# Sums over places in the pair selection: from folds on VectorE to matmuls with scaled identities on TensorE

## The chip, the cores and the metric

The kernel runs on one core of a Trainium2 chip. The metric is the device time of one execution in microseconds; before the change the median of three runs is 3086.44 us (3086.29 to 3088.57). The engines are named as in the profile: PE is TensorE (PEld its weight loads), DVE is VectorE, ACT is ScalarE, POOL is GpSimd, SP is SyncE, which here only issues DMAs.

## The reference

Two layers of an encoder on 512 tokens of width 1024. Each layer has two kinds of attention, a projection, a layer norm, and then a feed-forward part (PEER) that picks 16 of 16384 one-neuron experts for each token and each of 8 heads. The change touches only this choice:

```python
q = (xc @ wq).reshape(PEER_CHUNK, PEER_HEADS, 2, half)
sc = jnp.einsum('chpd,hpnd->chpn', q, sub_keys, preferred_element_type=jnp.float32)
s1, i1 = lax.top_k(sc[:, :, 0], PEER_TOPK)
s2, i2 = lax.top_k(sc[:, :, 1], PEER_TOPK)
cand = (s1[..., :, None] + s2[..., None, :]).reshape(...)
top_s, pos = lax.top_k(cand, PEER_TOPK)
eidx = jnp.take_along_axis(cidx, pos, axis=-1)
g = jax.nn.softmax(top_s, axis=-1)
```

Each chosen position `pos` among the candidate pairs has to be turned back into two key numbers, i1 and i2.

## The kernel before

The 512 tokens are four chunks of 128. Chunks 1, 2, 3 are "dense" (the experts of a chunk are spread into a table G in DRAM and all experts are computed), chunk 0 is "gathered" (experts fetched by indirect DMA). `order` is 1, 2, 3, 0. In a layer the work runs so:

- Attention; then the queries of the first two chunks together (`sub_keys`, generator `one`), of the third dense chunk (`two`, from `start(1)`) and of chunk 0 (`start(2)`). For each of 8 heads PE computes two queries `ps_pq` (8 fp32 matmuls of 128x128 for a single chunk; the trace has two records for each of them), ACT copies them out (`pq`, L478), PE multiplies them with the keys (`ps_ps`, L443), ACT copies the scores (`psc`, L446). For a dense chunk DVE then takes the best 16 keys of each half (`top_keys`: L496, L498, L501, here "a head").
- The pair selection `top_pairs` of each dense chunk, on DVE with two copies by ACT: 50 candidate sums (`cd`), the best 16 of them (`ts`, `pu`), and then the turning back. `ge` (16 places x 128, fp16) says for each place whether `pos` reaches the place's offset; `t` holds the steps `df` between the key numbers (copied wide by ACT, L563). Their product (L570) summed over the 16 places is i1. The sum is `fold`: three halvings and a last addition (L510, L511). `ge` times a table of steps (L575), folded, gives the offset `of` (L578); a comparison of `of` with the places (L580) times the second key numbers `t` (ACT, L573; DVE, L582), folded, gives i2.
- `gates(c)` (L720 on): PE transposes the gates, i1 and i2 of a chunk (`ps_t`, L727); DVE splits the gates into halves gh and gl; ACT writes i1 and i2 transposed into `iT`.
- `spread`: 48 times, DVE builds one-hot tiles from `iT` (`o12`, `ah`, `al`: L819 to L821), PE multiplies them (`ps_g`, L830, L831: fp16 128x128), ACT copies into staging; between them PE has the first expert blocks (`ps_a`, L772).
- The main loop over 128 expert blocks (L776 to L781 and L964 to L966), PE-heavy, with chunk 0's gathers beside it.

The order of the instructions on each engine is fixed when the program is built: a scheduler puts them in place by a priority, which is the place where the code emits them, and by its own view of when operands are there. Each engine then works through its list. In the code before, `top_pairs(order[2])` is emitted ahead of `start(2)`, the queries of chunk 0. In both orders, as in the trace, the two layers have the same pattern; layer 1's events of this stage come 1524.7 us after layer 0's, and only layer 0 is shown.

Of the kernel before, what the change touches and what calls it, by code (L numbers as in the profile page):

```python
# [8 lines left out]
F32 = mybir.dt.float32  # L9
F32R = mybir.dt.float32r  # L10
F16 = mybir.dt.float16
# [7 lines left out]
P = 128  # L19
# [3 lines left out]
NC = S // P  # L23
L = 2
HD = 64
NE = 16384
NB = 128
PH = 8
TK = 16
J = PH * TK  # L30
# [9 lines left out]
NCAND = [TK // (a + 1) for a in range(TK)]  # L40
# [5 lines left out]
def encoder_kernel(ctx: ExitStack, tc: tile.TileContext, x, ln_in_g, ln_in_b, w_in, qn_g, kn_g, sink,  # L46
# [12 lines left out]
    cp = ctx.enter_context(tc.tile_pool(name="cp", bufs=1))  # L59
# [8 lines left out]
    def acc_bank(nm):  # L68
        return ps.tile([P, 512], F32, tag="acc", name=nm, bufs=6)
# [5 lines left out]
        return ap.to_broadcast(shape)  # L75

    h = cp.tile([P, NC, D], F32, name="h")
    i1f = cp.tile([P, NC, J], F16, name="i1f")
    i2f = cp.tile([P, NC, J], F16, name="i2f")
    gte = cp.tile([P, NC, J], F32, name="gte")  # L80

    def rsqrt(src, scale, eps, n, nm):

# [64 lines left out]
    ident = cp.tile([P, P], F32, name="ident")  # L148
# [4 lines left out]
    v.tensor_copy(iota2, iota4.rearrange("p (n t) -> p n t", t=4)[:, :, 0:2])  # L153
    look = cp.tile([P, 3, TK, 8], F16, name="look")
    nc.sync.dma_start(look.rearrange("p a k j -> p (a k j)"), look_c)
    cos = cp.tile([P, NC, HD], F32, name="cos")
    sin = cp.tile([P, NC, HD], F32, name="sin")
    dist = cp.tile([P, 384], BF16, name="dist")
# [3 lines left out]
    for l in range(L):  # L162
# [41 lines left out]
        order = dense + gat  # L204
# [81 lines left out]
        st = {}  # L286
# [220 lines left out]
        def fold(t, dst):  # L507

            for n in (8, 4, 2):
                v.tensor_tensor(out=t[:, :n, :], in0=t[:, :n, :], in1=t[:, n:2 * n, :], op=ADD)  # L510
            v.tensor_tensor(out=dst, in0=t[:, 0, :], in1=t[:, 1, :], op=ADD)  # L511

        def pair_tiles():
            def small(tag, shape, dt):
                return pt.tile(shape, dt, tag=tag, name=tag, bufs=1)
            return dict(cd=small("cd", [P, PH, NCD], F32), ts=small("ts", [P, PH, TK], F32),
                        pu=small("pu", [P, PH, TK], U32), pos=small("pos", [P, J], F16),
                        xf=small("xf", [P, 2, PH, TK], F16), df=small("df", [P, PH, TK], F16),
                        of=small("of", [P, J], F16),
                        ge=pt.tile([P, TK, J], F16, tag="ge", name="ge"), t1=pt.tile([P, TK, J], F16, tag="t1", name="t1"))  # L520

        def pair_steps(st, c, tl):
# [33 lines left out]
            def table(i):  # L556
                return bc(look[:, i, :, None, :], b8)
# [11 lines left out]
            yield  # L569
            v.tensor_tensor(out=t1, in0=t1, in1=ge, op=MUL)  # L570
            yield
            fold(t1, i1f[:, c, :])
            act.copy(t1v, per_head(xf[:, 1]))  # L573
            yield
            v.tensor_tensor(out=gev, in0=gev, in1=table(1), op=MUL)  # L575
            yield
            fold(ge, of)
            v.tensor_tensor(out=of, in0=pos, in1=of, op=SUB)  # L578
            yield
            v.tensor_tensor(out=gev, in0=wide(of), in1=table(2), op=EQ)  # L580
            yield
            v.tensor_tensor(out=t1, in0=t1, in1=ge, op=MUL)  # L582
            yield
            fold(t1, i2f[:, c, :])
            yield
            gs = sm.tile([P, PH], F32, tag="gs", name="gs")
            v.tensor_reduce(out=gs, in_=gc, axis=AX.X, op=ADD)
# [7 lines left out]
        tks = {}  # L595
        xTs = {}

        groups = order[:2], order[2:3], order[3:]
# [121 lines left out]
        def gates(c):  # L720

            b = acc_bank("ps_t")
            i12 = ga.tile([P, 2, P], F32, tag="i12", name="i12", bufs=1)
            v.tensor_copy(i12[:, 0], i1f[:, c, :])
            v.tensor_copy(i12[:, 1], i2f[:, c, :])
            for i, src in enumerate((gte[:, c, :], i12[:, 0], i12[:, 1])):
                pe.transpose(b[:, i * P:(i + 1) * P], src, ident)  # L727
# [4 lines left out]
            iT = ga.tile([P, P // 8, 2, 8], F16, tag="iT", name="iT", bufs=3)  # L732
# [4 lines left out]
            act.copy(iT.rearrange("p o a t -> p a o t"), b[:, P:3 * P].rearrange("p (a o t) -> p a o t", a=2, t=8))  # L737
            flat[c] = gh, glf, gl, iT
# [140 lines left out]
        for c in gat:  # L879
# [3 lines left out]
            def rank(c=c, idx=idx, fx=fx):  # L883
                sx = slot()
                n = 2 * PH * TK
                st = {k: t.rearrange("p (a h k) -> p a h k", a=2, h=PH)
                      for k, t in (("sv", sx[:, :n]), ("ix", sx[:, n:2 * n].bitcast(U32)))}
                sc = []
                for i in range(2):
                    t = slot().rearrange("p (h a n) -> p h a n", a=2, n=P)  # L890
                    nc.sync.dma_start(t, Q[:, i * 4:(i + 1) * 4])
                    sc.append(t)
                yield
                for hd in range(PH):
                    yield from top_keys(st, hd, sc[hd // 4][:, hd % 4])
                big = [slot() for _ in range(3)]
                tl = dict(ge=big[0].bitcast(F16), t1=big[1].bitcast(F16))
                tl = {k: t.rearrange("p (a j) -> p a j", a=TK) for k, t in tl.items()}
                o = 0
                for k, shp, dt in (("cd", [PH, NCD], F32), ("ts", [PH, TK], F32), ("pu", [PH, TK], U32), ("pos", [J], F16),  # L900
                                   ("xf", [2, PH, TK], F16), ("df", [PH, TK], F16), ("of", [J], F16)):
                    n = math.prod(shp) // (2 if dt == F16 else 1)
                    t = big[2][:, o:o + n]
                    t = t if dt == F32 else t.bitcast(dt)
                    ax = "abc"[:len(shp)]
                    if len(shp) > 1:
# [4 lines left out]
                v.tensor_scalar(fx, i1f[:, c, :], 128.0, float(l * NE), op0=MUL, op1=ADD)  # L911
                v.tensor_tensor(out=idx, in0=fx, in1=i2f[:, c, :], op=ADD)  # L912
# [185 lines left out]
```

## Time and profile before

| | |
|---|---|
| median of three runs | 3086.44 us |
| the profiled execution | 3086.3 us |
| its span in the trace | 3084.5 us |
| PE busy | 2989.5 us (97%) |
| DVE busy | 2453.0 us (80%) |
| ACT busy | 1311.1 us (43%) |

A line of a timeline gives start, busy time, engine, source line, output <- input, shapes, count, and in brackets the idle time ahead of it with what ended it. Busy times on PE include a pipelined end, so the step from one start to the next is what an instruction takes in a row of its kind. [...]

### The profile page before, as it was taken

The page shows a single profiled execution, that of the slowest core. Times are in us where ns is not written, and L with a number is a line of the kernel's source. Part 1 is how long each engine was busy: PE and PEld are TensorE (multiplying, and loading weights), DVE is VectorE, ACT ScalarE, POOL GpSimd, SP SyncE. Part 2 cuts the span into 40 slices and gives each one's busy share as a digit, 9 for nine tenths or more (in the row PEclk, how much of TensorE's full clock was granted, in tenths as well). Part 3 has the DMA queues.
Part 4 walks back from the last instruction along what each step waited for, and adds up shares of the span by engine and source line. Part 5 has one row for each costly group of instructions (what it writes and reads, how often), then busy time and mean ns, then how long its engine had stood idle before and what let it go on. Part 6 is the DMA issues. An engine that isn't in the chain of part 4 may idle for free. (4 is left out here: it accounts for less than half of the span.)

```text
span 3084.5 us, 47606 instructions
## 1 busy us (share of the span) xinstructions
PE 2989.5 (97%) x17858; PEld 2704.7 (88%) x17858; DVE 2453.0 (80%) x5207; ACT 1311.1 (43%) x2586; POOL 748.8 (24%) x524
## 2 busy tenths in 40 slices
PE   6999899999999999999999999999999999999998
PEld 6989887899999999999888888779999999999997
DVE  6777999678777777877777779987787787787777
ACT  2664268343333333333347532773433333333332
POOL 0000000014444444444000000000244344444540
PEclk9999999999999999999999999999999999999999
DMA  4113567659888888888520236675698988888882
GB/s 178 42 56 129 212 232 287 219 199 333 317 322 313 320 318 313 320 317 314 189 96 15 71 132 244 245 290 179 246 334 305 325 315 313 322 317 311 324 311 92
DMA packets 262232, 749.46 MB, mean 243 GB/s; under 512 B 19952, under 2 KB 130288, under 8 KB 231792
## 3 DMA queue, kind: packets, MB, share of 16 engines
q1 hardware_dynamic: 188272, 477.94, 42.8%
q0 software_dynamic: 73728, 268.47, 24.1%
q8 instruction: 140, 2.29, 0.3%
q14 instruction: 92, 0.75, 0.1%
HBM read 691.81 MB, written 54.53 MB: 242 GB/s over the span
## 5 line engine op out<-in xcount | busy, mean ns | idle before, releaser
L921 POOL DMA_INDIRECT gt<-in_dram,idx x512 | 742.3, 1450 | 2062.7 <-DVE idx L912 1197.7
L779 PE MATMUL ps_a<-xTh,uh 128*128 128x384 f32 x1824 | 610.6, 335 | 3.7 <-ACT uh L776 3.7
L781 PE MATMUL ps_a<-xTh,ul 128*128 128x384 f32 x1824 | 612.2, 336 | 0.0
L780 PE MATMUL ps_a<-xTl,uh 128*128 128x384 f32 x1824 | 610.8, 335 | 0.0
L966 PE MATMUL ff<-vh,wl 128*128 128x512 f32 x1476 | 576.4, 391 | 0.0
L964 PE MATMUL ff<-vh,wh 128*128 128x512 f32 x1476 | 574.9, 389 | 0.0
L965 PE MATMUL ff<-vl,wh 128*128 128x512 f32 x1476 | 574.5, 389 | 0.0
L997 ACT CAST vh<-vt 128x1024 fp32r<-128x1024 f32 x246 | 258.5, 1052 | 607.8 <-PE ff L966 308.1
L998 DVE TENSOR_TENSOR vl<-vt,vh 128x1024 fp32r<-128x1024 f32 x246 | 301.2, 1224 | 195.8 <-ACT vh L997 194.7
L779 PEld LDWEIGHTS ps_a<-xTh,uh 128*128 128x128 f32 x1824 | 342.7, 188 | 14.4 <-ACT uh L776 5.6
L780 PEld LDWEIGHTS ps_a<-xTl,uh 128*128 128x128 f32 x1824 | 342.6, 188 | 10.4
L927 DVE CUSTOM_DVE_ANT_0 junk<-gt,h 128x1024 bf16<-128x1024 f32 x256 | 313.1, 1223 | 37.6 <-DMA gt<-in_dram,idx 33.0
L781 PEld LDWEIGHTS ps_a<-xTh,ul 128*128 128x128 f32 x1824 | 342.5, 188 | 0.1
L1004 ACT CAST wh<-w 128x384 fp32r<-128x384 f32 x246 | 126.3, 513 | 478.3 <-DVE w L1001 474.3
L938 DVE SCALAR_TENSOR_TENSOR gacc<-gt,gw,gacc 128x1024 f32<-128x1024 f32 x252 | 311.6, 1280 | 21.3 <-DMA gt<-in_dram,idx 21.3
L966 PEld LDWEIGHTS ff<-vh,wl 128*128 128x128 f32 x1476 | 277.2, 188 | 57.6
L964 PEld LDWEIGHTS ff<-vh,wh 128*128 128x128 f32 x1476 | 277.0, 188 | 49.6 <-ACT wh L1004 0.9
L965 PEld LDWEIGHTS ff<-vl,wh 128*128 128x128 f32 x1476 | 277.2, 188 | 48.6
L777 DVE TENSOR_TENSOR ul<-ut,uh 128x1024 fp32r<-128x1024 f32 x228 | 277.9, 1219 | 21.7 <-ACT uh L776 21.7
L776 ACT CAST uh<-ut 128x1024 fp32r<-128x1024 f32 x228 | 239.7, 1052 | 121.8 <-PE ps_a L780 120.5
L1005 DVE TENSOR_TENSOR wl<-w,wh 128x384 fp32r<-128x384 f32 x246 | 137.5, 559 | 158.9 <-ACT wh L1004 158.9
L772 PE MATMUL ps_a<-xTd,ut 128*128 128x384 f32 x448 | 156.1, 493 | 0.0
(261 smaller groups left out, 4857.4 us busy)
## 6 DMA issues: line engine op xcount, KB each, us to landing
ut<-in_dram SPq DMA_DIRECT2D x128, 1024.0 KB, 8.4
vt<-in_dram SPq DMA_DIRECT2D x128, 1024.0 KB, 7.2
w_pq<-in_dram SPq DMA_DIRECT2D x48, 1024.0 KB, 5.0
gg<-G SPq DMA_DIRECT2D x62, 768.0 KB, 13.8
G<-stg SPq DMA_DIRECT2D x24, 1920.0 KB, 7.0
w_o<-in_dram SPq DMA_DIRECT2D x24, 1024.0 KB, 4.8
w_q<-in_dram SPq DMA_DIRECT2D x8, 1024.0 KB, 6.3
gt<-in_dram,idx POOLq DMA_INDIRECT x512, 7.3
```

Source lines behind the costliest of these rows:

```text
L777: v.tensor_tensor(out=ul.rearrange(ff), in0=us, in1=uh.rearrange(ff).bitcast(F32), op=SUB)
L779: pe.matmul(b[:, :ND], uh[:, k, :], xTh[:, k, :], start=k == 0, stop=False)
L780: pe.matmul(b[:, :ND], uh[:, k, :], xTl[:, k, :], start=False, stop=False)
L781: pe.matmul(b[:, :ND], ul[:, k, :], xTh[:, k, :], start=False, stop=k == KD - 1)
L921: pool.indirect_dma_start(out=t, out_offset=None, in_=src, in_offset=bass.IndirectOffsetOnAxis(ap=idx[:, j:j + 1], axis=0))
L927: v.tensor_tensor_reduce(out=jk, in0=t, in1=h[:, c, :], op0=MUL, op1=ADD, scale=1.0, scalar=0.0, accum_out=a_[:, j:j + 1])
L938: v.scalar_tensor_tensor(acc[j % 2], t, w_[:, j:j + 1], acc[j % 2], op0=MUL, op1=ADD)
L964: pe.matmul(b, wh[:, cs], vh[:, ns], start=blk == 0, stop=False)
L965: pe.matmul(b, wh[:, cs], vl[:, ns], start=False, stop=False)
L966: pe.matmul(b, wl[:, cs], vh[:, ns], start=False, stop=blk == NB - 1)
L997: act.copy(vh, vt[:, bi, :])
L998: v.tensor_tensor(out=vl, in0=vt[:, bi, :], in1=vh.bitcast(F32), op=SUB)
```

## The change

For dense chunks the folds go. Seven identities scaled by 1, 2, 3, 4, 5, 8 and 16 are made once at the start (`idw`, fp16). `sum_places` lets PE add the 16 places: 16 matmuls with a place of `t` as weights and the identity as the moving side, into one PSUM tile `ps_f`, which comes out transposed, so that ACT copies it straight into `iT_all`. For `of` 15 matmuls with scaled identities as weights and places of `ge` as the moving side replace the product with the table and its fold. `t2` is a second buffer beside `t1`. The matmuls are emitted at a priority lowered by 400 for the first two chunks and not lowered for the third; the third selection is emitted behind `start(2)`. The transposes of i1 and i2 in `gates` go with the two casts ahead of them. Chunk 0 keeps the old code.

```diff
+    steps_ = [0] + NCAND[:-1]
+    idw = {k: cp.tile([P, P], F16, name=f"id{k}") for k in sorted(set(steps_) - {0})}
+    for k, t in idw.items():
+        v.tensor_scalar(t, ident, float(k), None, op0=MUL)
...
+        def sum_places(t, i, iT, late):
+
+            b = acc_bank("ps_f")
+            with tc.high_priority(offset=-late):
+                for a in range(TK):
+                    pe.matmul(b[:, :P], t[:, a, :], idw[1], start=a == 0, stop=a == TK - 1)
+            act.copy(iT[:, :, i, :], b[:, :P].rearrange("p (o t) -> p o t", t=8))
...
-            fold(t1, i1f[:, c, :])
+            if iT is not None:
+                sum_places(t1, 0, iT, late)
+                b = acc_bank("ps_f")
+                with tc.high_priority(offset=-late):
+                    for a in range(1, TK):
+                        pe.matmul(b[:, :P], idw[steps_[a]], ge[:, a, :], start=a == 1, stop=a == TK - 1)
+                v.tensor_tensor(out=of, in0=pos, in1=b[:, :P], op=SUB)
+                t1 = tl["t2"]
...
+            else:
+                fold(t1, i1f[:, gat.index(c), :])
             act.copy(t1v, per_head(xf[:, 1]))
...
-            fold(t1, i2f[:, c, :])
+            if iT is not None:
+                sum_places(t1, 1, iT, late)
...
         def top_pairs(c):
-            for _ in pair_steps(tks[c], c, pair_tiles()):
+            iTs[c] = iT_all[:, dense.index(c)]
+            for _ in pair_steps(tks[c], c, pair_tiles(), iTs[c], 0 if c == order[2] else 400):
                 pass
...
-        top_pairs(order[2])
         for _ in start(2):
             pass
+        top_pairs(order[2])
         gates(order[2])
```

How the order moves, at three places of layer 0. First PE, in the queries of the third chunk (`two`): here is the program before, where `tr_x0` are the transposes of chunk 0 and `ps_pq` the queries.

```order
L443 MATMUL ps_ps_4282<-keys_4185,pq_4265 128x128
L472 MATMUL ps_pq_4297<-xT1_3674,w_pq_4227 128x128 x8
L129 MATMUL tr_x0_4395<-ident_81,h_69 128x128 x4
L129 MATMUL tr_x0_4401<-ident_81,h_69 128x128 x4
L472 MATMUL ps_pq_4411<-xT1_3674,w_pq_4268 128x128 x8
```

The same place now; `t1_4331` and `t2_4332` are the first chunk's products, `ps_f_4427` the sum that gives its i2.

```order
L534 LDWEIGHTS t1_4331
L534 MATMUL ps_f_4389<-id1_90,t1_4331 128x128
L534 LDWEIGHTS t2_4332
L534 MATMUL ps_f_4427<-id1_90,t2_4332 128x128
L130 MATMUL tr_x0_4450<-ident_82,h_69 128x128 x4
L130 MATMUL tr_x0_4456<-ident_82,h_69 128x128 x4
L478 MATMUL ps_pq_4466<-xT1_3689,w_pq_4283 128x128 x8
L534 LDWEIGHTS t2_4332
```

Of the 16 matmuls of the i2 sum one stands ahead of the transposes and of the queries, 15 behind them; all 31 of the first chunk's other two sums stand ahead as well. Farther down the second chunk's i2 sum stands the same way: one matmul ahead of the query `ps_pq_4618`, 15 much later.

Second DVE, where `t2_4332` is written: now the product stands behind the fourth head of the third chunk (`psc_4480`), and behind all candidates of the second chunk; the second chunk's product, `of`, comparison and product follow in one piece.

```order
L606 TENSOR_TENSOR ge_4330<-of_4329,look_88 128x2048
L504 MAX_INDEX ix_3869<-sv_3868,psc_4480 128x8
L608 TENSOR_TENSOR t2_4332<-t2_4332,ge_4330 128x2048
L560 CAST pos_4495<-pu_4494 128x128
L616 TENSOR_REDUCE gs_4614<-gte_72 128x8
L583 TENSOR_TENSOR ge_4499<-pos_4495,look_88 128x2048
L617 RECIPROCAL gs_4614<-gs_4614 128x8
L585 TENSOR_TENSOR t1_4500<-t1_4500,ge_4499 128x2048
L618 TENSOR_TENSOR gte_72<-gte_72,gs_4614 128x128
L593 TENSOR_TENSOR of_4498<-pos_4495,ps_f_4576 128x128
L606 TENSOR_TENSOR ge_4499<-of_4498,look_88 128x2048
L608 TENSOR_TENSOR t2_4501<-t2_4501,ge_4499 128x2048
```

Before, the first chunk's product stood behind the second head, and the second chunk's candidates behind it.

```order
L498 MAX_INDEX ix_3854<-sv_3853,psc_4244 128x8 x2
L580 TENSOR_TENSOR ge_4315<-of_4314,look_87 128x2048
L589 TENSOR_TENSOR gte_72<-gte_72,gs_4390 128x128
L582 TENSOR_TENSOR t1_4316<-t1_4316,ge_4315 128x2048
L496 MAX sv_3853<-psc_4285 128x8 x2
```

Third PE, at the end of chunk 0's queries (`xT2`): the third chunk's sums come behind the last query.

```order
L478 MATMUL ps_pq_5040<-xT2_4449,w_pq_4992 128x128 x8
L449 MATMUL ps_ps_5051<-keys_4991,pq_5032 128x128
L534 LDWEIGHTS t1_5065
L534 MATMUL ps_f_5123<-id1_90,t1_5065 128x128
L534 LDWEIGHTS t1_5065
L534 MATMUL ps_f_5123<-id1_90,t1_5065 128x128
L592 LDWEIGHTS id16_96
L592 MATMUL ps_f_5141<-ge_5064,id16_96 128x128
L449 MATMUL ps_ps_5051<-keys_4991,pq_5049 128x128
```

Behind them come, in this order, five and then ten matmuls left of the second chunk's i2 sum, the third chunk's i2 sum, the transpose of its gates, the 24 transposes `tr_x` and the spread. In ACT's list the wide copy of the third chunk's `df` stands in the middle of chunk 0's query copies, between `pq_4861` and `pq_4876`.

## Rows read from the trace of the kernel before

**Rows 1.** The page: the chain that ended last, by engine.

```profile
PE 32%; DVE 0%; ACT 0%; DVEq 0%; issue 0%
```

**Rows 2.** Windows of 10 us in the stage of the selections, layer 0.

```profile
370.00:380.00 10.00, 7.46 (x67) 7.27 (x66) 10.00 (x91) 0.88 (x3) 0.00 (x0) 1.00 0.95 359
380.00:390.00 10.00, 7.29 (x46) 6.86 (x47) 10.00 (x27) 5.09 (x10) 0.00 (x0) 0.83 0.34 119
```

**Rows 3.** Who waited for whom from 330 to 415 us, for PE and for ACT: total, times, longest.

```profile
PE ps_ps L443 <- ACT pq L478: 4.5, 1, 4.5
PE ps_t L727 <- DVE i L724: 1.4, 1, 1.4
...
ACT t L563 <- DVE df L549: 20.7, 3, 10.0
```

**Rows 4.** Timeline of DVE: the third chunk's turning back.

```profile
412.45 0.68 DVE L510 TENSOR_TENSOR t<-t 128x1024 f16<-128x1024 f16 x1
413.05 1.22 DVE L575 TENSOR_TENSOR ge<-ge,look 128x2048 f16<-128x2048 f16 x1
414.19 0.42 DVE L510 TENSOR_TENSOR t<-t 128x512 f16<-128x512 f16 x1
414.52 0.69 DVE L510 TENSOR_TENSOR ge<-ge 128x1024 f16<-128x1024 f16 x1
415.12 0.29 DVE L510 TENSOR_TENSOR t<-t 128x256 f16<-128x256 f16 x1
415.33 0.42 DVE L510 TENSOR_TENSOR ge<-ge 128x512 f16<-128x512 f16 x1
415.66 0.22 DVE L511 TENSOR_TENSOR i1f<-t 128x128 f16<-128x128 f16 x1
415.80 0.29 DVE L510 TENSOR_TENSOR ge<-ge 128x256 f16<-128x256 f16 x1
416.00 0.20 DVE L588 RECIPROCAL gs<-gs 128x8 f32<-128x8 f32 x1
...
416.46 0.22 DVE L578 TENSOR_TENSOR of<-pos,of 128x128 f16<-128x128 f16 x1
...
418.06 1.23 DVE L582 TENSOR_TENSOR t<-t,ge 128x2048 f16<-128x2048 f16 x1
419.32 1.48 DVE L510 TENSOR_TENSOR t<-t 128x1024 f16<-128x1024 f16 x3
```

**Rows 5.** Timeline of DVE: the start, the gap that the identities fall into, and the two ends of the stretch in which DVE does the first chunk's turning back, the layer norm of chunk 0, the second chunk's candidates and four heads.

```profile
21.65 2.36 DVE L217 TENSOR_TENSOR wlo<-w_k,whi 128x1024 fp32r<-128x1024 f32 x2 [3.50 <-ACT whi L216]
...
350.18 0.28 DVE L587 TENSOR_REDUCE gs<-gte 128x8 f32<-128x128 f32 x1
...
379.40 0.22 DVE L549 TENSOR_TENSOR df<-xf 128x120 f16<-128x120 f16 x1
379.54 0.22 DVE L545 CAST pos<-pu 128x128 f16<-128x128 uint32 x1
```

**Rows 6.** Timeline of PE: queries and keys of the third chunk from the transposes on, the long wait, and the end of chunk 0's queries with the first of the spread's fp16 matmuls.

```profile
362.58 1.04 PE L129 MATMUL tr_x<-ident,h 128*128 128x128 f32 x8
363.45 1.95 PE L472 MATMUL ps_pq<-xT,w_pq 128*128 128x128 f32 x16
365.24 0.61 PE L443 MATMUL ps_ps<-keys,pq 128*128 128x128 f32 x4
365.69 3.74 PE L472 MATMUL ps_pq<-xT,w_pq 128*128 128x128 f32 x32
...
381.97 1.24 PE L443 MATMUL ps_ps<-keys,pq 128*128 128x128 f32 x4 [4.51 <-ACT pq L478]
383.00 3.10 PE L472 MATMUL ps_pq<-xT,w_pq 128*128 128x128 f32 x16
385.94 0.39 PE L443 MATMUL ps_ps<-keys,pq 128*128 128x128 f32 x2
...
424.55 2.78 PE L129 MATMUL tr_x<-ident,h 128*128 128x128 f32 x24
427.17 0.22 PE L830 MATMUL ps_g<-ah,o 128*128 128x128 f16 x1
...
428.03 0.22 PE L831 MATMUL ps_g<-al,o 128*128 128x128 f16 x1
```

**Rows 7.** Short waits of PE elsewhere (timeline).

```profile
44.44 1.09 PE L129 MATMUL tr_h<-ident,h 128*128 128x128 f32 x8 [2.18 <-DVE h L116]
54.21 1.91 PE L129 MATMUL tr_h<-ident,h 128*128 128x128 f32 x8 [2.19 <-DVE h L116]
...
320.31 0.92 PE L129 MATMUL tr_o<-ident,o 128*128 128x128 f32 x4 [2.63 <-DVE o L378]
```

**Rows 8.** Windows of 1 us of PE alone behind those waits (columns: stretch, length, PE busy, granted clock, DMA share, GB/s).

```profile
45.00:46.00 1.00, 0.76 (x7) 1.00 0.00 0
...
55.00:56.00 1.00, 1.00 (x7) 0.50 0.44 180
...
322.00:323.00 1.00, 1.00 (x7) 0.50 0.02 8
```

**Rows 9.** A window of the spread, with all engines, and from the timeline of PE the expert blocks behind its end.

```profile
440.00:480.00 40.00, 40.00 (x347) 29.27 (x345) 39.10 (x52) 32.86 (x76) 0.00 (x0) 1.00 0.71 279
...
540.28 7.96 PE L772 MATMUL ps_a<-xTd,ut 128*128 128x384 f32 x24
```

More of the change, by code (lines that the diff above doesn't have):

```diff
@@ L77, in encoder_kernel @@
     h = cp.tile([P, NC, D], F32, name="h")
-    i1f = cp.tile([P, NC, J], F16, name="i1f")
-    i2f = cp.tile([P, NC, J], F16, name="i2f")
+    i1f = cp.tile([P, len(gat), J], F16, name="i1f")
+    i2f = cp.tile([P, len(gat), J], F16, name="i2f")
     gte = cp.tile([P, NC, J], F32, name="gte")
+    iT_all = cp.tile([P, len(dense), P // 8, 2, 8], F16, name="iT_all")
     def rsqrt(src, scale, eps, n, nm):
@@ L519, in pair_tiles, with pair_steps @@
                         of=small("of", [P, J], F16),
-                        ge=pt.tile([P, TK, J], F16, tag="ge", name="ge"), t1=pt.tile([P, TK, J], F16, tag="t1", name="t1"))
-        def pair_steps(st, c, tl):
+                        ge=pt.tile([P, TK, J], F16, tag="ge", name="ge"),
+                        **{k: pt.tile([P, TK, J], F16, tag=k, name=k, bufs=1) for k in ("t1", "t2")})
+        def sum_places(t, i, iT, late):
[4 more added lines that the diff above has]
+            act.copy(iT[:, :, i, :], b[:, :P].rearrange("p (o t) -> p o t", t=8))
+        def pair_steps(st, c, tl, iT=None, late=0):
             sv, ix = st["sv"], st["ix"]
@@ L571, in pair_steps @@
             yield
-            fold(t1, i1f[:, c, :])
+            if iT is not None:
[6 more added lines that the diff above has]
+                t1 = tl["t2"]
+                t1v = t1.rearrange("p a (h k) -> p a h k", h=PH)
+            else:
+                fold(t1, i1f[:, gat.index(c), :])
             act.copy(t1v, per_head(xf[:, 1]))
             yield
[L575 to L579, printed above, removed]
+            if iT is None:
+                v.tensor_tensor(out=gev, in0=gev, in1=table(1), op=MUL)
+                yield
+                fold(ge, of)
+                v.tensor_tensor(out=of, in0=pos, in1=of, op=SUB)
+                yield
             v.tensor_tensor(out=gev, in0=wide(of), in1=table(2), op=EQ)
@@ L583, in pair_steps @@
             yield
-            fold(t1, i2f[:, c, :])
+            if iT is not None:
+                sum_places(t1, 1, iT, late)
+            else:
+                fold(t1, i2f[:, gat.index(c), :])
             yield
@@ L591, in top_pairs @@
         def top_pairs(c):
-            for _ in pair_steps(tks[c], c, pair_tiles()):
+            iTs[c] = iT_all[:, dense.index(c)]
+            for _ in pair_steps(tks[c], c, pair_tiles(), iTs[c], 0 if c == order[2] else 400):
                 pass
         tks = {}
+        iTs = {}
         xTs = {}
@@ L722, in gates @@
             b = acc_bank("ps_t")
[L723 to L727, printed above, removed]
+            pe.transpose(b[:, :P], gte[:, c, :], ident)
             gT = ga.tile([P, P], F32, tag="gT", name="gT", bufs=1)
@@ L731, in gates @@
             gl = ga.tile([P, P], F16, tag="gl", name="gl", bufs=3)
-            iT = ga.tile([P, P // 8, 2, 8], F16, tag="iT", name="iT", bufs=3)
             v.tensor_scalar(gT, b[:, :P], GS, None, op0=MUL)
@@ L736, in gates @@
             v.tensor_copy(gl, glf)
-            act.copy(iT.rearrange("p o a t -> p a o t"), b[:, P:3 * P].rearrange("p (a o t) -> p a o t", a=2, t=8))
-            flat[c] = gh, glf, gl, iT
+            flat[c] = gh, glf, gl, iTs[c]
         for c in order[:2]:
             gates(c)
-        top_pairs(order[2])
         for _ in start(2):
             pass
+        top_pairs(order[2])
         gates(order[2])
@@ L910, in rank @@
                 yield from pair_steps(st, c, tl)
-                v.tensor_scalar(fx, i1f[:, c, :], 128.0, float(l * NE), op0=MUL, op1=ADD)
-                v.tensor_tensor(out=idx, in0=fx, in1=i2f[:, c, :], op=ADD)
+                v.tensor_scalar(fx, i1f[:, gat.index(c), :], 128.0, float(l * NE), op0=MUL, op1=ADD)
+                v.tensor_tensor(out=idx, in0=fx, in1=i2f[:, gat.index(c), :], op=ADD)
             ranks = rank()
```

## The prediction

> **What bounds the kernel now.** I read four views, in this order. The chain of waits first: all of it that the profile can place is PE [rows 1], so what counts is when PE gets through its list. Then windows of 10 us over the stage of the selections, where the change lies. From 370 to 400 us DVE is busy for the whole of each window and PE is not: 7.46 and 7.29 of 10 us, and in the second the granted clock is 0.83 on average [rows 2]. So this is a stage where DVE is full and PE waits now and then. The list of waits says for what: once 4.5 us for a query copy of ACT, which itself stood behind a wide copy waiting for DVE's `df` (three such waits, 20.7 us on ACT), and 1.4 us for the cast of i1, with ready queries behind the waiting transpose [rows 3]. That second row is the one to keep in mind: an instruction of PE that waits holds all that stands behind it. Last, the timelines of PE and DVE [rows 4 to 6], from which the sum is made. Behind the stage nothing gives time back: in the spread PE is busy 40.00 of 40 us with DVE at 39.10, and when DVE is through, PE still has 7.96 us of expert blocks [rows 9]. A delay of PE at the first `ps_g` (427.17 [rows 6]) should reach the end whole, once per layer.
>
> **What the change takes from DVE.** A fold steps 0.60, 0.33, 0.21 and 0.14: 1.28 us for the one of i1; the one of `of` 0.60, 0.33, 0.20 and 0.14, 1.27 [rows 4]. The product with the table is 1.14 (413.05 to 414.19). Per dense chunk three folds and this product go: 3 x 1.27 + 1.14 = 4.95 us, and two casts. The seven identities are made once, ahead of the 3.50 us in which DVE waits for a cast of ACT [rows 5]; seven times about 0.2 us, the size of the small rows in [rows 4], is 1.4, so that gap hides them; uncovered they would cost 1.4 once.
>
> **What it gives to PE.** Per dense chunk 16 + 15 + 16 = 47 fp16 matmuls of 128x128. The nearest rows are the `ps_g`: 15 steps from 427.17 to 428.03, 0.0573 us each [rows 6], so 31 sums are 1.78 us and 16 are 0.92. [...]
>
> **Where the sums stand, which decides.** Walk PE's new list from the point where it is unchanged, 362.58 us in layer 0 [rows 6].
>
> 1. Ahead of the transposes now stand two `ps_ps` (0.45, by 365.24 to 365.69), the first chunk's 31 sums (1.78), and one weight load of `t2`. PE comes to it at 364.8.
> 2. That load needs DVE's product `t2`, which now stands behind the second chunk's candidates and four heads. Before, DVE works without a gap from 350.18 to 379.54 [rows 5] and does the same pieces plus three folds and one table product of the first chunk. So the product ends at 379.54 - 4.95 + 0.2 (one small subtraction that comes earlier now) = 374.8. PE waits 10.0 us. Behind it stand eight transposes and all remaining queries, which need nothing from this product, and behind the transposes the copies that feed chunk 0's queries.
> 3. PE resumes at half clock. After the 4.51 us wait the four `ps_ps` and 16 query records took 3.97 us (381.97 to 385.94), against 0.45 + 1.79 at full speed [rows 6]: 1.73 lost. Then 0.87 (eight transposes) + 1.79 (a query of 16 records) + 0.92 + 0.22 + 1.73 = 5.5: 380.3. The second chunk's 31 sums: 382.1.
> 4. Again one matmul of an i2 sum (second chunk) stands ahead of the queries. `of`, comparison and product now follow the sums directly on DVE: 2.86 us (416.46 to 419.32 [rows 4]), nothing beside them on PE. 385.0.
> 5. To the last key product: 23 queries of 1.79, 23 `ps_ps` of 0.225, two transposes: 46.6 us. In it ACT's copy of the third chunk's `df` stands ahead of query copies, as it did in the 4.51 us wait. Bounds 0 and 4.5; I take 1, since PE has seven queries (12.5 us) to do before it needs a copy from behind it. 432.6.
> 6. The third chunk's selection is now behind the queries: 31 sums and five left over (2.06), again 2.86 for DVE with ten leftover sums in its shade, then 16 sums, 25 transposes (0.92 + 0.11 + 2.62, the last by 424.55 to 427.17): 441.2.
>
> So the first `ps_g` comes at 441.2 instead of 427.17, 14.0 us later, although the old waits and the old half-clock stretch are gone from this walk. Two terms are left open: whether the waits of 2.86 us and of about 2.3 us (2.86 less the ten sums) also halve the clock. Of three such waits elsewhere, 2.18 us was followed by full clock, 2.19 and 2.63 by 0.50 [rows 7, 8]. Each costs 0 or 1.73; I take three of the four in two layers. [...]
>
> Sum: 2 x 14.0 + 3 x 1.73 = 33.2 us. The profiled execution took 3086.3 us (span 3084.5), within 0.2 us of the median, so 3119.5; I say 3119.
>
> **Rivals.** First, faster: PE is not held, and DVE's 4.95 us per chunk end the waits. For it: DVE is full just where PE waits [rows 2], and the long wait of [rows 6] does go back to DVE's `df` [rows 3]. Its price: the same walk without steps 2's and 4's waits and without half clock, 362.58 + 0.45 + 1.78 + 3.80 + 1.78 + 46.6 + 2.06 + 2.86 + 3.65 = 425.6, 1.6 a layer earlier, 3083. It is little because the sums are 8.1 us of new PE work per layer, about as much as the waits that go. It decides when `t2` is there before PE asks for it, that is when DVE is through at 364.8 instead of 374.8; the work in front of it, four heads and the second chunk's candidates, speaks against.
>
> Second, no change: the wait only moves. PE loses now 4.51 + 1.4 + some short ones and 1.73 of clock; if the product came at about 367 the new waits would be as long. That asks for 8 us less on DVE than [rows 5] give.
>
> Third, the change doesn't do what it says: the lowered priority is meant to leave the queries first, and in the built order one matmul of a sum stands ahead of them twice. That is the forecast itself.
>
> [...]
>
> **Numbers.** The forecast, two waits in which PE is held per layer, 0.90, as the step from the fixed order to the wait needs no unknown cost; the faster rival 0.05; no change 0.05. Its own bounds: low, the held product 3 us earlier and no half clock at all: 14.0 - 1.7 - 3 = 9.3 a layer, 3105; high, the fourth case, 3127. I give 3103 to 3129 and leave the two rivals outside. A measurement of this kernel tells 0.2% (6.2 us) from no change. Faster 0.05, same 0.05, slower 0.90.
>
> **What would show it.** In the changed trace: PE's idle time ahead of a weight load of `t2` near 365 us, 10 us long, released by DVE's product, and the same 1524.7 us or a little more later in layer 1; a half-clock stretch behind it; a second wait of near 2.9 us ahead of the second chunk's single matmul; the sums at 0.057 us; the first `ps_g` at 441 to 445; DVE no longer full from 385 to 432. Against it: no idle time there (then DVE's stretch was mis-sized or PE went past the load), or a `ps_g` as late but a spread that ends as early as before (then the spread has slack that I deny).

## The result, and the profile after

The changed kernel takes 3129.14 us (median of four executions, 3128.25 to 3130.83) against 3087.51 for the kernel before (four executions): a ratio of 1.0135, 95% interval 1.0121 to 1.015, 41.6 us slower. The forecast was slower, 3119 us; the range of 3103 to 3129 ends 0.14 us below the measured median. The profiled execution of the changed kernel took 3130.83 us, its span is 3129.1; PE is busy for 3017.7 us of it, 28.2 more than before, DVE for 2425.3, 27.7 less.

The list of waits from 330 to 460 us in layer 0 (engine, tile and line, what it waited for; total, times, longest), PE and DVE, in the place of [rows 3]:

```profile
DVE of L593 <- PE ps_f L592: 24.7, 2, 20.1
PE ps_f L534 <- DVE t L608: 11.0, 3, 4.6
DVE sv L502 <- ACT psc L452: 10.8, 4, 5.9
...
PE ps_ps L449 <- DMA keys<-in_dram: 3.5, 2, 3.3
...
DVE t L608 <- ACT t L598: 1.2, 1, 1.2
```

PE no longer waits for a cast, and for a query copy only once, 0.35 us. It waits three times for the product `t` of an i2 sum, and 3.25 us for keys, a wait that is new. DVE, which was busy for the whole of the windows from 370 to 390 us before, now waits 24.7 us for sums. The timeline of PE in the same stage, against [rows 6] (the sums and a key product between are left out):

```profile
363.40 1.95 PE L478 MATMUL ps_pq<-xT,w_pq 128*128 128x128 f32 x16
368.60 0.77 PE L449 MATMUL ps_ps<-keys,pq 128*128 128x128 f32 x2 [3.25 <-DMA keys<-in_dram]
...
377.81 0.29 PE L534 MATMUL ps_f<-id,t 128*128 128x128 f16 x1 [4.61 <-DVE t L608]
377.90 1.92 PE L130 MATMUL tr_x<-ident,h 128*128 128x128 f32 x8
379.60 2.61 PE L478 MATMUL ps_pq<-xT,w_pq 128*128 128x128 f32 x16
...
388.32 0.29 PE L534 MATMUL ps_f<-id,t 128*128 128x128 f16 x1 [2.97 <-DVE t L608]
388.40 5.14 PE L478 MATMUL ps_pq<-xT,w_pq 128*128 128x128 f32 x32
393.38 0.39 PE L449 MATMUL ps_ps<-keys,pq 128*128 128x128 f32 x2
```

Both single matmuls are there, each with transposes or queries right behind it. The clock in these stretches (stretch, length, busy time of PE, PEld, DVE, ACT, POOL, granted clock of PE as a share of full speed, DMA share, GB/s):

```profile
366.00:374.00 8.00, 4.61 (x35) 4.25 (x35) 8.00 (x66) 1.39 (x4) 0.00 (x0) 0.58 0.99 389
374.00:377.00 3.00, 0.00 (x0) 0.00 (x0) 3.00 (x12) 1.31 (x1) 0.00 (x0) 0.50 0.14 57
377.00:381.00 4.00, 3.19 (x16) 3.19 (x17) 3.76 (x7) 1.17 (x2) 0.00 (x0) 0.50 0.00 0
...
388.00:390.00 2.00, 1.68 (x9) 1.69 (x9) 0.26 (x1) 0.00 (x0) 0.00 (x0) 0.50 0.00 0
```

And the end of the stage in layer 0: last of chunk 0's key products, the third chunk's sums, transposes, the first `ps_g` (427.17 before); then the same end in layer 1.

```profile
437.96 0.44 PE L449 MATMUL ps_ps<-keys,pq 128*128 128x128 f32 x2
...
444.21 0.40 PE L534 MATMUL ps_f<-id,t 128*128 128x128 f16 x4 [3.42 <-DVE t L608]
...
445.69 2.35 PE L130 MATMUL tr_x<-ident,h 128*128 128x128 f32 x20
448.60 0.91 PE L797 MATMUL ps_a<-xTd,ut 128*128 128x384 f32 x2 [0.56 <-ACT xTd L135]
449.35 0.28 PE L855 MATMUL ps_g<-ah,o 128*128 128x128 f16 x2
...
1989.64 0.61 PE L534 MATMUL ps_f<-id,t 128*128 128x128 f16 x4 [3.42 <-DVE t L608]
...
1992.39 3.86 PE L130 MATMUL tr_x<-ident,h 128*128 128x128 f32 x20
...
1997.24 0.28 PE L855 MATMUL ps_g<-ah,o 128*128 128x128 f16 x2
```

To compare kernels, one stretch of layer 0 is used below, called the stage: from the end of the third chunk's 8th query (362.58 before; in the changed kernel 363.40 + 1.79 = 365.19) to the first matmul of the main loop's kind, which reads `uh` (549.75 before, 571.11 now; before and after, PE's timeline).

```profile
549.75 0.44 PE L779 MATMUL ps_a<-xTh,uh 128*128 128x384 f32 x1 [1.51 <-ACT uh L776]
571.11 0.44 PE L804 MATMUL ps_a<-xTh,uh 128*128 128x384 f32 x1 [1.51 <-ACT uh L801]
```

It takes 187.2 us before and 205.9 after: 18.7 us more in layer 0. In layer 1 (1909.85 to 2119.01) it takes 209.2, 22.0 more. The two stages make 40.7 of the 44.6 us by which the profiled execution's span is longer (3129.1 less 3084.5). The rest lies ahead of them, 2.6 us ahead of the first and 1.2 between the two; behind the second nothing is lost or won (1010.06 us to the end in both kernels).

### The profile page after: what moved, and what is told of

The parts are those of the page before. It is cut to its first block, busy times and chain, and to the rows that moved or that the text cites. A ratio compares the mean times of both kernels' runs of the same rounds, so it can differ in the third digit from the quotient of the medians.

```text
span 3129.1 us, 48073 instructions
## 1 busy us (share of the span) xinstructions
PE 3017.7 (96%) x18128; PEld 2729.9 (87%) x18128; DVE 2425.3 (78%) x5124; ACT 1313.8 (42%) x2592; POOL 740.2 (24%) x524
## 3 DMA queue, kind: packets, MB, share of 16 engines
q0 software_dynamic: 73728, 268.47, 23.9%
## 5 line engine op out<-in xcount | busy, mean ns | idle before, releaser
L946 POOL DMA_INDIRECT gt<-in_dram,idx x512 | 733.5, 1433 | 2114.3 <-DVE idx L937 1240.4
```

What stands on the lines that cost most here:

```text
L946: pool.indirect_dma_start(out=t, out_offset=None, in_=src, in_offset=bass.IndirectOffsetOnAxis(ap=idx[:, j:j + 1], axis=0))
```

## The experiments

All times are medians; each ratio is to the kernel before, run on the same chip.

| run | us | ratio, 95% interval | stage, layer 0, us |
|---|---|---|---|
| before | 3087.5 | 1 | 187.2 |
| the changed kernel | 3129.1 | 1.0135 (1.0121 to 1.015) | 205.9 |
| e1 third selection early | 3154.75 | 1.0217 (1.0199 to 1.0234) | 221.2 |
| e2 move alone, folds | 3086.11 | 0.9996 (0.9987 to 1.0006) | 187.2 |
| e3 no hold, third last | 3110.46 | 1.0076 (1.006 to 1.0093) | 199.1 |
| e4 no hold, third between | 3092.34 | 1.0014 (1.0004 to 1.0024) | 189.1 |
| e5 e4, wide copy later | 3081.41 | 0.9979 (0.9969 to 0.9988) | 184.6 |
| e6 folds, order by hand | 3095.05 | 1.0024 (1.0014 to 1.0034) | 191.0 |
| e7 sums for chunks 1 and 3 | 3090.28 | 1.001 (1.0 to 1.0019) | 188.1 |
| e8 two buffers of t2 | 3127.65 | 1.0127 (1.011 to 1.0144) | 206.1 |
| e9 e7, gates later | 3078.21 | 0.9968 (0.9956 to 0.9981) | 182.2 |
| e10 e5, third's sums last | 3090.34 | 1.0013 (1.0003 to 1.0023) | 190.7 |
| e11 e5, one matmul ahead | 3103.96 | 1.0054 (1.0037 to 1.0071) | 193.7 |
| e12 e6, gates later | 3079.72 | 0.9975 (0.9966 to 0.9985) | 183.9 |

**The two parts of the change, one at a time.** e1 undoes the place of the third selection, e2 does only that (the same move in the kernel before).

```diff
+        top_pairs(order[2])
         for _ in start(2):
             pass
-        top_pairs(order[2])
```

> The changed kernel with one part undone: the third selection is emitted ahead of chunk 0's queries again; the sums stay on TensorE. In the built order 15 + 31 + 16 sums of the second and third chunk now stand ahead of chunk 0's 16 queries. Theory H (PE is held by sums that stand ahead of queries and wait for DVE's products): PE is through the third chunk's queries at about 404 us and then waits for the third chunk's first product (419.3 in the changed kernel's trace), its second product 3 us behind the sums, and has all 16 queries (32 us) still to do: first ps_g near 463 instead of 449.4, about 14 us a layer worse, 3157 us (3145 to 3165). Rival T (the loss comes from the third selection standing behind all queries, with 11.6 us of tail in which nothing else runs): the tail goes, about 9 us a layer better, 3111 us.

> The kernel before with one part alone: the third selection is emitted behind chunk 0's queries, all sums stay folds on VectorE. H: the built order is that of before but for one ACT instruction per layer (the exponential of the gates), so no change, 3087 us within 3. T: a tail of about 9 us a layer as in the changed kernel, 3105 us.

e1 came out at 3154.75, with the first `ps_g` at 463.00 where 463 was expected. Its timeline of PE shows the sums of the third chunk ahead of all of chunk 0's queries:

```profile
418.71 0.39 PE L534 MATMUL ps_f<-id,t 128*128 128x128 f16 x2 [14.01 <-DVE t L585]
424.86 0.96 PE L534 MATMUL ps_f<-id,t 128*128 128x128 f16 x8 [2.90 <-DVE t L608]
463.00 0.22 PE L855 MATMUL ps_g<-ah,o 128*128 128x128 f16 x1
```

e2 is no change, and its stage is as long as before. In its trace PE and DVE run the same instructions in the same order as before; only the exponential of the gates on ACT has moved, once per layer. So the place in the code alone moves nothing, and e2 can't tell what a late third selection with folds would cost. Rival T, that the place of the third selection makes the loss, gave 3111 for e1 and falls there: with the third selection early the kernel is 25.6 us slower still. What the late place costs is measured by e10 below.

e2 also bears on what lies ahead of the stage. With the same order on PE its first `ps_k`, the first matmul of the kernel's attention, comes 0.24 us earlier than before (21.43 against 21.67), and yet its transposes of chunk 0 begin 1.46 us later (364.04 against 362.58). The 2.6 us by which the profiled execution of the changed kernel comes late to the stage look like the same kind of difference between executions: 1.5 of them are there at the first `ps_k` (23.20), while e1, e3 and e8, which make the same identities, start it at 21.57 to 21.69, and e3 and e4 come to the transposes at 361.87 and 361.89.

**The hold taken away.** In e3 the sums stay on PE, but the lists of PE and ACT are written by hand in this stage: `go(g, n)` emits n queries, `until(s, mark)` a selection up to a mark ahead of its wide copy ("wide"), its 31 sums ("sums") or its i2 sum ("i2"). e4 also spreads the third selection between chunk 0's queries.

```diff
...
-        top_pairs(order[0])
+        by_hand = tc.manual_schedule(engines={mybir.EngineType.PE, mybir.EngineType.Activation})
+        by_hand.__enter__()
+        one_ = begin_pairs(order[0])
+        until(one_, "sums")
         for half in range(2):
             flip_x(2, 0, half)
-        next(two)
-        top_pairs(order[1])
+        go(two, 1)
+        until(one_, "i2")
+        two_ = begin_pairs(order[1])
+        until(two_, "wide")
+        go(two, 2)
+        until(two_, "sums")
+        go(two, 3)
+        until(one_, "end")
+        go(two, 1)
+        until(two_, "i2")
         for _ in two:
             pass
...
+        zero_ = start(2)
+        go(zero_, 2)
+        until(two_, "end")
...
```

What e4 changes in e3:

```diff
-        for _ in zero_:
-            pass
         top = begin_pairs(order[2])
+        until(top, "wide")
+        go(zero_, 6)
+        until(top, "sums")
+        go(zero_, 3)
+        until(top, "i2")
+        go(zero_, 3)
         until(top, "end")
+        for _ in zero_:
+            pass
```

> The changed kernel with the same sums on TensorE and the third selection still last, but the lists of PE and ACT in this stage written out by hand: the 31 sums of the first chunk behind the 9th query of the third chunk, its i2 sum behind the 14th, the second chunk's 31 sums behind the 15th, its i2 sum behind the second query of chunk 0; the wide copy of the second chunk's steps behind the 11th query. H: the waits ahead of the first and second chunk's i2 sums and the half clock behind them go, the first ps_g comes near 430 us where the changed kernel has 446.8 (without its later start of 2.6), 17 us a layer, 3095 us; if the wait for the keys and its half clock stay, 3105. T: the tail stays and makes most of the loss, no better than 3118.

> As e3, and the third selection spread between chunk 0's queries: its wide copy behind the 8th, its 31 sums behind the 11th, its i2 sum behind the 14th. H: no hold and no tail: 417 us (the walk without waits up to the last key product) + 3.6 (sums of the second and third chunk that come later) + 2.7 (transposes) = 423.4 for the first ps_g against 427.2 before, 3080 us; with a wait for keys and its half clock left, 3090. T: the same as H here. A rival to both, that the 8.1 us of sums on PE per layer cost more than the waits that go: 3095 or more.

e3 took 3110.46, 18.7 us less than the changed kernel, and e4 3092.34. Both missed H's figures, 3095 and 3080, by 15 and 12 us. H allowed 3105 and 3090 if the wait for keys stayed, but that wait is down to 0.6 us in both, so something else is left; between H and the rival of e4 (3095 or more) this pair doesn't decide. The traces name what is left. In e3:

```profile
378.37 0.80 PE L449 MATMUL ps_ps<-keys,pq 128*128 128x128 f32 x2 [2.79 <-ACT pq L484]
...
427.08 1.89 PE L534 MATMUL ps_f<-id,t 128*128 128x128 f16 x16 [3.52 <-DVE t L587]
...
433.54 1.89 PE L534 MATMUL ps_f<-id,t 128*128 128x128 f16 x16 [2.97 <-DVE t L611]
```

The first is new and comes from the order by hand: query copies stand behind ACT's wide copy of the second chunk's `df`, as they did in the kernel before [rows 3]. It is in e4 too. The other two are the tail. e5 puts that wide copy two queries later, and the second chunk's sums with it:

```diff
         until(two_, "wide")
-        go(two, 2)
+        go(two, 4)
         until(two_, "sums")
-        go(two, 3)
-        until(one_, "end")
         go(two, 1)
-        until(two_, "i2")
+        until(one_, "end")
         for _ in two:
             pass
+        until(two_, "i2")
...
-        go(zero_, 2)
+        go(zero_, 4)
         until(two_, "end")
...
         until(top, "wide")
-        go(zero_, 6)
+        go(zero_, 4)
```

> e4 with ACT's wide copy of the second chunk's steps behind the 13th query of the third chunk instead of the 11th, the second chunk's 31 sums behind the 16th query and its i2 sum behind the fourth of chunk 0 (both later, so that no new wait comes). Theory H (in e4 the rest of the loss is PE's wait of 2.79 us for query copies that stand behind this wide copy, and the half clock behind it, 4.2 us a layer): first ps_g at 424.5 where e4 has 428.8, 3084 us. Rival S (the 8.1 us of sums per layer are the loss): no better than 3090.

3081.41, faster than before. No wait of PE above 0.60 us is left in this stretch of its trace. So the same sums on PE that made the kernel 41.6 us slower leave it 6.9 us faster than before when PE's and ACT's lists are put so that ready work doesn't stand behind a sum or a copy that isn't ready. Rival S falls.

**The hold and the tail put back one at a time, from e5.** e11 sends one matmul of the first chunk's i2 sum ahead of the transposes (the sum is split behind its first matmul by a mark "rest", which is not shown; one copy of ACT, of the second key numbers, moves ahead of the transposes' copies with it); e10 puts the third chunk's sums behind all queries.

```diff
-        for half in range(2):
-            flip_x(2, 0, half)
-        go(two, 1)
         until(one_, "i2")
         two_ = begin_pairs(order[1])
         until(two_, "wide")
+        until(one_, "rest")
+        for half in range(2):
+            flip_x(2, 0, half)
+        go(two, 1)
```

```diff
-        go(zero_, 4)
+        go(zero_, 6)
         until(top, "sums")
-        go(zero_, 3)
-        until(top, "i2")
-        go(zero_, 3)
-        until(top, "end")
         for _ in zero_:
             pass
+        until(top, "end")
```

> e5 with the hold put back and nothing else: the first matmul of the first chunk's i2 sum stands ahead of chunk 0's transposes and of the third chunk's 9th query, as in the changed kernel; its other 15 stay behind the 14th query. In the built order VectorE's product t2 stands behind three heads here (four in e5 and in the changed kernel), one head, about 3 us, earlier than 374.8. H: PE comes to the one weight load at about 365 and waits 7 us for the product, runs behind it at half clock (1.7 to 2.7 us), and nothing gives it back: 9 to 10 us a layer, 3100 us (3096 to 3106) against 3081.4. Rival (the hold itself is cheap because PE would wait for keys or VectorE later anyway): 3086 or less.

> e5 with the third chunk's 31 + 16 sums moved behind all queries, its product ready long before. H: against e5 only VectorE's step between the sums (a wait of 2.97 us as in the changed kernel) and the half clock behind it (1 to 1.5 us) are added, 4 to 4.5 us a layer, 3090; so of the changed kernel's loss the third selection's place makes about 9 us and the holds ahead of queries the rest. Rival T (the place behind the queries makes the loss): 3110 or more.

With this one matmul moved on PE, e11 is 22.5 us slower than e5. PE's timeline in e11, layer 0 and layer 1:

```profile
372.60 0.29 PE L617 MATMUL ps_f<-id,t 128*128 128x128 f16 x1 [8.46 <-DVE t L611]
372.68 1.91 PE L130 MATMUL tr_x<-ident,h 128*128 128x128 f32 x8
374.39 2.51 PE L478 MATMUL ps_pq<-xT,w_pq 128*128 128x128 f32 x16
376.73 0.61 PE L449 MATMUL ps_ps<-keys,pq 128*128 128x128 f32 x4
...
1902.60 0.29 PE L617 MATMUL ps_f<-id,t 128*128 128x128 f16 x1 [8.45 <-DVE t L611]
1902.68 1.92 PE L130 MATMUL tr_x<-ident,h 128*128 128x128 f32 x8
1904.39 3.62 PE L478 MATMUL ps_pq<-xT,w_pq 128*128 128x128 f32 x16
1907.80 0.77 PE L449 MATMUL ps_ps<-keys,pq 128*128 128x128 f32 x4
```

The waits are 16.9 us. Transposes and query behind them, by the starts, take 1.71 + 2.34 and 1.71 + 3.41 instead of 0.87 + 1.79 each: 3.9 us of half clock (the granted clock is 0.50 from 372 to 374 us). Together 20.8 of the 22.5 (the two stages in the traces are 20.0 us longer than in e5). ACT's moved copy holds nothing: PE waits for the product alone, 8.5 of its 8.9 us. e10 lands where it was expected, 8.9 us above e5. In both layers PE waits 2.97 us; in layer 0 half clock follows (16 sums in 1.68 us instead of 0.90, 24 transposes in 4.6 instead of 2.6), and from the first sum to the first `ps_g` are 6.52 us, in layer 1 only 3.64 (last two rows):

```profile
425.53 1.89 PE L534 MATMUL ps_f<-id,t 128*128 128x128 f16 x16 [2.97 <-DVE t L611]
427.43 4.78 PE L130 MATMUL tr_x<-ident,h 128*128 128x128 f32 x24
432.05 0.22 PE L885 MATMUL ps_g<-ah,o 128*128 128x128 f16 x1
...
1951.69 1.07 PE L534 MATMUL ps_f<-id,t 128*128 128x128 f16 x16 [2.97 <-DVE t L611]
...
1955.33 0.22 PE L885 MATMUL ps_g<-ah,o 128*128 128x128 f16 x1
```

**The small wait in the tail.** In the changed kernel DVE's last product waits 1.22 us for ACT's copy, which begins at 441.00, behind two copies out of `ps_f`:

```profile
442.93 1.22 DVE L608 TENSOR_TENSOR t<-t,ge 128x2048 f16<-128x2048 f16 x1 [1.22 <-ACT t L598]
```

```diff
-                        **{k: pt.tile([P, TK, J], F16, tag=k, name=k, bufs=1) for k in ("t1", "t2")})
+                        **{k: pt.tile([P, TK, J], F16, tag=k, name=k, bufs=1 if k == "t1" else 2) for k in ("t1", "t2")})
```

> The changed kernel with two buffers for t2, nothing else. In its trace VectorE waits 1.22 us for ACT's copy of the third chunk's second key numbers, behind the queries. H: that copy waits because the one buffer of t2 is held by the second chunk's 15 leftover sums, which the lowered priority puts behind all queries; with two buffers it stands far ahead in ACT's list, the wait goes, 1.2 us a layer, 3126.7 us (an effect near what can be told; the wait itself is read from the trace). Rival: the wait is ACT's own queue (the copies out of ps_f), and stays.

The wait is gone, so it came from the buffer that the leftover sums hold, and not from ACT's queue:

```profile
438.83 1.22 DVE L608 TENSOR_TENSOR t<-t,ge 128x2048 f16<-128x2048 f16 x1
```

The time is 1.5 us lower, too little to tell. In layer 0 nothing was won at all (stage 206.1 against 205.9): PE's wait is 2.23 us instead of 3.42, but behind it the granted clock is 0.50 (440 to 442 us), where it was 1.00 in the changed kernel (444 to 446). In layer 1, where half clock followed in both (eight sums in 0.85 us instead of 0.45), the stage is 2.1 us shorter (207.1 against 209.2).

**Do the sums on PE pay at all?** e6 takes them all back to DVE and keeps the order by hand; e7 leaves them on PE for chunks 1 and 3. Both keep the second buffer `t2`, and both need the old transposes of i1 and i2 in `gates` for the folded chunks. From e7:

```diff
...
+    by_pe = [1, 3]
+    fl = [c for c in range(NC) if c not in by_pe]
...
-            iTs[c] = iT_all[:, dense.index(c)]
+            iTs[c] = iT_all[:, by_pe.index(c)] if c in by_pe else None
...
-        for c in order[:2]:
-            gates(c)
+        gates(order[0])
+        go(zero_, 2)
+        gates(order[1])
...
```

> All sums back as folds on VectorE (no scaled identities), but the lists of PE and ACT in this stage by hand as in e5: wide copies behind the 16th query of the third chunk and behind the 14th of chunk 0, the second key numbers in a buffer of their own, the transposes of i1 and i2 behind the 3rd and the 6th query of chunk 0. H: PE has no sums and none of the long waits, and would be through at 417; VectorE sets the end, the third chunk's i2 near 420.9 as before, first ps_g near 424, 3081 us (3076 to 3087). S: the order alone gives as much as or more than the sums on PE, e6 below e5. Rival V (VectorE's folds are what costs): e6 at 3087 or more, e5 clearly below.

> The order by hand with the sums on PE for the first and the third chunk, folds for the second. H: PE has 5.4 us of sums instead of 8.1, VectorE is through 10 us earlier than with folds alone: first ps_g near 420.5, 6.5 us a layer better than before, 3074 us (3070 to 3084, the upper end with one short wait and its half clock per layer).

Both missed, e6 at 3095.05 and e7 at 3090.28, by the same fault: the transposes of the gates, put between queries, wait for DVE. In e7 PE waits itself (first row, PE's timeline); in e6 PE waits for a query copy (second, the same view), which stands behind ACT's copy of `iT`, and this waits for DVE (third, ACT's timeline):

```profile
395.02 0.33 PE L786 MATMUL ps_t<-ident,gte 128*128 128x128 f32 x1 [3.09 <-DVE gte L627]
```

```profile
398.53 0.80 PE L450 MATMUL ps_ps<-keys,pq 128*128 128x128 f32 x2 [6.19 <-ACT pq L485]
```

```profile
397.93 0.37 ACT L795 CAST iT<-ps_t 128x256 f16<-128x256 f32 x1 [8.28 <-DVE gT L789]
```

e9 (from e7) and e12 (from e6) only move these transposes, in e9:

```diff
-        gates(order[1])
         top = begin_pairs(order[2])
...
         for _ in zero_:
             pass
+        gates(order[1])
         gates(order[2])
```

and in e12 the first chunk's as well, to behind chunk 0's 12th query.

> e7 with one thing moved: the transposes of the second chunk's gates, i1 and i2 behind all queries. In e7's trace PE waits 3.09 and 0.48 us for VectorE ahead of these transposes, with queries behind them, and runs a query at half clock behind the wait (3.2 instead of 1.8 us): 5.2 us a layer. H: they go, 3090.3 - 10 = 3080; against e5 two layers of 2.7 us of sums less on PE, 3077. Rival: VectorE is the bound with the second chunk's folds on it, a wait of the same size appears ahead of a later sum, no change, 3090.

> e6 with the transposes of the gates moved: the first chunk's behind the 12th query of chunk 0, the second chunk's behind all. In e6's trace ACT waits 8.28 us for VectorE's gT ahead of its copy of the first chunk's iT, query copies stand behind it, and PE waits 6.19 us for them: a fault of the order by hand, 7 to 8 us a layer. H: it goes; VectorE with all folds sets the end, the third chunk's i2 near 421, first ps_g near 424 to 425, 3081 us (3077 to 3087). Theory S (the order, not the sums on PE, is what beats the kernel before): e12 at 3082 or less, level with e5. Theory V (folds on VectorE cost what the sums on PE save): e12 at 3086 or more.

3078.21 and 3079.72. With the order by hand the folds alone are level with e5's sums on PE (3081.41), and two chunks' sums on PE are at best 1.5 us better than none; the ranges of single executions overlap (3075.82 to 3079.70 and 3077.84 to 3083.00). So theory S of e12 holds: the sums on PE aren't needed to beat the kernel before. The order by hand does it with the folds too, together with the second buffer of the key numbers, which e12 keeps and which was not taken away by itself. The sums are about an even trade in these two orders; neither order was tuned further, and e12 still has waits of PE of 1.62 and 2.04 us. In e12 DVE is full again from 370 to 410 us, and so is PE but for 0.19 us. e9 is the best version of this study, 0.9968 of the kernel before (0.9956 to 0.9981), 9.6 us. The first `ps_g` would have misled here: in e12 it comes at 428.07, later than before, because expert blocks stand ahead of it; the stage is 3.3 us shorter.

## Why the prediction was right or wrong

The direction, the mechanism and both places were right; the size was short. What failed is the sizing of the walk behind the holds, above all step 6, the tail from the last key product to the first `ps_g`, and step 5 ahead of it.

The forecast was 3086.3 + 33.2 = 3119.5, and the profiled execution took 3130.83, 11.3 us more. Of these 3.8 lie outside the two stages. The stages took 40.7 us more than before instead of 33.2; the 7.5 us go to the steps as follows, over both layers (the parts add up to 7.7, by rounding):

- **Step 2, the hold, was right.** The product comes 12.62 us after the start of the stage (377.81 less 365.19) where the walk had 12.2 (374.8 less 362.58), in layer 1 12.63. PE's own idle time ahead of it reads 4.61 instead of 10.0, because something not foreseen stood in front: 3.25 us for keys and 31 sums at half clock (0.50 from 368.6 to 374 us). Without them PE would only have waited longer, since DVE sets the product's time. e11 shows the same hold without the wait for keys.
- **Steps 3 and 4** were nearly right. The second wait is 2.97 in both layers (2.86 forecast). Half clock behind the first hold cost 1.5 us in layer 0 and 2.2 in layer 1 (1.73 forecast; granted clock 0.50 from 377 to 381 and from 1922 to 1926 us), behind the second 1.4 and 1.7 (0.50 from 388 to 390 and from 1935 to 1937). From the start of the stage to the second chunk's single matmul are 23.1 and 23.9 us where the walk had 22.4: with step 2 some 2.2 us of the 7.5.
- **Step 5.** From 388.32 to the end of the last key product at 438.40 are 50.1 us, 1.4 of them half clock, which the forecast priced apart; the walk had 47.6. Some 1 us per layer was missing, 1.9 in all. The 1 us put in for a query copy behind ACT's wide copy was 0.35; the rest is other small waits (0.27 for keys among them) that the walk did not contain.
- **Step 6, the tail, is the step that failed most.** The walk gave 8.6 us from the last key product to the first `ps_g`. It is 10.95 in layer 0 (438.40 to 449.35) and 13.4 in layer 1, 2.46 more, where the granted clock is 0.50 (1990 to 1994 us; 1.00 from 444 to 449 in layer 0). Missing were, in each layer, the 1.22 us that the one buffer of `t2` costs (e8), 0.56 us (0.24 in layer 1) of waiting for ACT's `xTd`, and an expert block of 0.75 us that the scheduler put ahead of the spread. The block is work that only comes earlier and is not lost; without it the tail is short by some 1.6 us a layer, 3.2 of the 7.5.
- **The clock.** Of the four short waits three were followed by half clock, as taken; they cost 1.4, 1.7 and 2.46 instead of 1.73 each, 0.4 us more together. That it was three of four is a count that no rule of the prediction gave, so its fit is partly luck.
- **The high end.** 3127, the fourth case of the range, was the 28 us of the walk (2 x 14.0), 6.9 for half clock behind all four short waits (4 x 1.73), and a wider spacing of the sums than that of [rows 6]. No run shows such a spacing: the sums ran at 0.056 us each (e5: 16 of them from 368.96 to 369.86) and at 0.107 at half clock (the changed kernel, 370.01 to 372.89). Waits that the walk did not contain were not in it. So the high end came near the result for a reason that did not occur: what filled the gap was the terms above.
- **Upstream.** The 3.8 us outside the stages, 2.6 of them ahead of the first, are most likely not the change (e2, e3, e4); the profiled execution is also the slowest of the four, 1.7 us above their median. The median lies 0.14 us above the range; the four executions differ by up to 2.6 us.

Put together from e5 (3081.4): the tail 8.9 (e10), one matmul ahead of the transposes 22.5 (e11), which makes 3112.8. The rest, 16.3 us, was not run apart and is an estimate from the changed kernel's trace: the second chunk's hold with its half clock, 2 x 2.97 + 1.4 + 1.7 = 9.0; the first hold, longer by the one head more that stands ahead of the product in the changed kernel, (12.62 less the 2.2 of two key products and 31 sums) less 8.46 = 1.9 a layer, 3.9 in all; 1.5 for the buffer, which is within the noise. That leaves 1.9.

The rivals: the faster one priced a kernel without holds, but with the third selection behind all queries, at 3083. e10 comes closest to that kernel, and took 3090.3. e5 came to 3081.4, but without the tail, so that it is near 3083 by chance. The lowered priority did not keep all sums behind the queries: 15 matmuls of each of the first two chunks' i2 sums did stand behind a query, and the first one ahead of it. Why the scheduler sent that one ahead was not tested. DVE did stop being full, as forecast: 24.81 of 47 us from 385 to 432, against 43.06 before.

```profile
385.00:432.00 47.00, 43.53 (x375) 42.77 (x372) 24.81 (x156) 11.52 (x34) 0.00 (x0) 0.96 0.72 246
```

## What to carry to other kernels

An engine that works through a fixed list is held by the first instruction that isn't ready, however low its priority was (22.5 us here for one matmul, e11); when work moves to the engine that bounds the kernel, look in the built order for the one instruction that stands ahead of ready work, and price it by when its operand comes. Before moving work between engines to end waits, try the order alone: here, with one more buffer, it gave within 1.5 us as much as the move at its best, and the gain lay in putting each copy, transpose and sum behind enough ready work. Compare kernels by a mark at which the moved work has all been done, not by the first instruction of the next stage.

## What the runs showed of the hardware that I had not expected

- The length of a wait does not settle the clock behind it in these traces. The wait of 3.42 us in the tail of the changed kernel was followed by a granted clock of 1.00 in layer 0 (444 to 449 us) and of 0.50 in layer 1 (1990 to 1994), and with it the way to the first `ps_g` took 5.14 us (444.21 to 449.35) against 7.60 (1989.64 to 1997.24). In e8 a wait of 2.23 us was followed by 0.50 in layer 0 (440 to 442). In e10 a wait of 2.97 us was followed by 6.52 us to the first `ps_g` in layer 0 and by 3.64 for the same work in layer 1. So waits of 2.23 and 2.97 us cost clock here, and one of 3.42 did not.

```profile
444.00:446.00 2.00, 1.79 (x24) 1.00 0.01 4
```

```profile
440.00:442.00 2.00, 1.89 (x16) 0.50 0.02 6
```

(PE alone, the changed kernel above, e8 below; the columns are those of [rows 8].)

- A load that is hardly slower than before can still hold PE, when the new order asks for it earlier. The keys of the new 3.25 us wait are those issued at 361.42 in the changed kernel; before, those of the same place were issued at 357.78, landed 6.8 us after their issue and were used at 365.24 without a wait. The trace of the changed kernel has no landing for its load, but from its issue to the end of PE's wait at 368.60 are 7.18 us, so the load took at most 0.4 us longer than before. What moved more is both ends: the key products now stand right behind the 8th query, where eight transposes and a query, 2.66 us, stood between, and the load was issued 3.77 us ahead of the start of the stage instead of 4.80. In e8, with the same order here, PE waits 3.14 us at this place. Below: the issue before and in the changed kernel (SP's timeline), then the wait in e8 (PE's).

```profile
357.78 0.42 SPq L425 DMA_DIRECT2D keys<-in_dram  x1
...
361.42 0.43 SPq L431 DMA_DIRECT2D keys<-in_dram  x1
...
365.53 0.77 PE L449 MATMUL ps_ps<-keys,pq 128*128 128x128 f32 x2 [3.14 <-DMA keys<-in_dram]
```
